# One-bank PSUM tiles in merging, four places for the decay weights, and earlier loads, in a hybrid encoder on one Trainium2 core

## The chip, the cores and the metric

The program runs on one core of a Trainium2 chip. The core has TensorE (PE, matrix products, with a separate sequence of weight loads, PEld), VectorE (DVE), ScalarE (ACT), GpSimd (POOL) and SyncE (SP), which here issues nearly all DMA transfers. The engines run their own instruction streams in order and wait for each other through semaphores. The metric is the device time of one execution in microseconds (us).

## What is computed

One layer of an encoder on 1024 prompt tokens and 256 sample tokens, with 1024 channels:

```python
h = rms_norm(x, norm_g) * (1.0 + scale) + shift          # scale, shift, gate from c @ w_ada
cb, cc, cx, cz, q, k, v, o, mz, gpre, gmerge = split_combined(h @ w_in)
y_conv = cb * centred_dwconv3(cc * cx, conv_w, conv_b) * silu(cz)
hm = mlstm_chunkwise(q, k, v, forward gates) + the same backward     # 4 heads of 256, chunks of 128
y_m = sigmoid(o) * head_rms_norm(hm) * silu(mz)
merged = g_conv * (y_conv @ w_proj_conv) + g_mlstm * (y_m @ w_proj_mlstm)   # gates: sigmoid(gmerge)
y = rms_norm(x + gate * (merged @ w_out), final_norm_g)
```

## The kernel before, in words

Matrix products run in fp32r with both factors split into a high and a low part: a product is three matmuls, high by high, high by low and low by high. ScalarE casts the high part of a weight (`wh`, from a loaded `raw` tile), and GpSimd subtracts it for the low part (`wl`); in the first stage that is L320 and L321, in the second L1665 and L1666.

The order of all work is planned on the host by a small class, `Board`. Code appends operations with an engine, an estimated cost, what they read and write, and sometimes marks: `low` (a load or product that goes behind the others), `slack` (its planned start is put later by so much). `order()` plans start times, at 230 KB/us for loads and a fixed landing time, and `play()` emits the instructions in the order of the planned starts. So one edit moves instructions on engines that it does not touch. Buffers of a pool are handed out in turn. Dependencies follow whole tiles: an engine that writes any part of a PSUM tile waits for a pending read of any other part.

There are four stages. (1) Up to about 1163 us the input projection (`go`, L810), by Strassen's scheme; results leave PSUM through `q` tiles on VectorE (L719). Within it the gates' recurrences and the decay weights of the mLSTM are worked out. `weights(i)`, called for 20 pieces, takes a `big` tile, loads two rows of log weights broadcast to all partitions (`big<-a_dr`, 256 KB), adds a mask on GpSimd (L1246), exponentiates on ScalarE (four times, L1250) and stores the result for the sweeps. (2) Up to about 1444 us the sweeps over the mLSTM's chunks (classes `Sweep` and `Pairs`). They leave gaps on TensorE, which `Filler` fills with the convolution branch's projection: 16 blocks of 128 channels and 640 tokens, two units each, of 24 matmuls 128x320 (L1707 to L1709). `load_w` loads raw weights for two blocks, `split` makes `wh` and `wl`, and VectorE multiplies the accumulator by the gate tile `th` (L620, inside `times_1p`). `load_head(h, n)` loads piece n of a head's `vN`, `qT` and `kT`. (3) Up to about 1566 us merging (`merge`): 16 blocks, two groups of 24 matmuls (L1883 to L1885) each. VectorE takes the group out of PSUM by L620 with a gate tile `th`, and adds the convolution's part (`zc`, L1891). At its beginning the second half of the mLSTM's output is loaded and split, on VectorE by L1850. (4) The output projection, again by Strassen's scheme, in two quads of token tiles and a last pair (class `Tokens`, products L1975 to L1977), with the norm at the end. PSUM has eight banks of 512 floats per partition; merging and the output have them as four tiles of two banks (`psD` one, `psO` three).

Of the kernel before, what the change touches and what calls it, by code (L numbers as in the profile page):

```python
# [182 lines left out]
def encoder_kernel(  # L183
# [1055 lines left out]

    def weights(i):  # L1240

        gx = gcol[:, 0].rearrange("p d h c -> p d (h c)")
        place = big()
        abc = (lambda: place[:, 0:4 * P].rearrange("p (d j s) -> p d j s", d=2, j=2))
        load(256, abc, a_rows[:, 2 * i:2 * i + 2, :].partition_broadcast(P), ["a_dr"], [place])
        op("POOL", 1.35, lambda: G.tensor_tensor(out=abc(), in0=abc(), in1=masks[:].unsqueeze(2).to_broadcast([P, 2, 2, P]),  # L1246
                                                 op=ALU.add), r=[place], w=[place])
# [5 lines left out]
        store(256, ex_dr[i], lambda: place[:, 0:4 * P], [place])  # L1253
# [172 lines left out]
    def load_head(h, n, which="qkv"):  # L1426

        i, (c0, c1) = h % 2, PIECES[n]
        hs, ts_ = slice(h * HD, (h + 1) * HD), slice(c0 * P, c1 * P)
        kb = 128 * (c1 - c0)  # L1430
        if "v" in which:
            load(kb, lambda: vNs[i][:, c0:c1, 0:HD], v_dr[ts_, hs].rearrange("(c p) d -> p c d", p=P), (), [(vNs[i], n)], h > 0)
        for nm, t, src in (("q", qTs[i], qT_dr), ("k", kTs[i], kT_dr)):
            if nm in which:
                load(kb, lambda t=t: t[:, :, ts_], src[hs, ts_].rearrange("(b p) t -> p b t", p=P), (), [(t, n)], h > 0)
# [207 lines left out]
    class Filler:  # L1643
# [36 lines left out]
        def unit(self, after):  # L1680
# [66 lines left out]
    for s in range(10 * NH + 15):  # L1747
# [62 lines left out]
    banks = []  # L1810

    def bank():
        k = len(banks)
        if k % 2 == 0:
            banks.append(buf(*((psO, [P, 2, 512], F32, "acc", 3) if k % 8 < 6 else (psD, [P, 2, 512], F32, "acc", 1))))
        else:
            banks.append(banks[-1])
        b = banks[-1]
        return (lambda: b[:, k % 2]), (b, k % 2)
# [48 lines left out]
    def merge(i, y):  # L1868
# [6 lines left out]
        for q in range(2):  # L1875
# [3 lines left out]
            def mm(part, acc=acc, qs=qs):  # L1879
                for kt in range(2 * part, 2 * part + 2):  # L1880
                    wh, wl = (w[:, kt % 4, :] for w in ws[kt // 4])
                    yH, yL = (t[:, kt % 4, qs] for t in y[kt // 4])
                    PE.matmul(acc()[:, :TQ], wh, yH, start=kt == 0, stop=False)  # L1883
                    PE.matmul(acc()[:, :TQ], wh, yL, start=False, stop=False)  # L1884
                    PE.matmul(acc()[:, :TQ], wl, yH, start=False, stop=kt == KT - 1)  # L1885
# [4 lines left out]
            op("DVE", .48, lambda acc=acc, qs=qs: times_1p(th[:, qs], th[:, qs], acc()[:, :TQ]), r=[tok, (th, q)], w=[(th, q)])  # L1890
# [15 lines left out]
    class Tokens:  # L1906
# [73 lines left out]
        def banks(self, pool):  # L1980
            b = buf(pool, [P, 2, 512], F32, "acc", 1 if pool is psD else 3)
            return [((lambda j=j: b[:, j]), (b, j)) for j in range(2)][:self.n]

        def copy_out(self, dst, tag):

            t = o_tile(tag)
            for j in range(self.n):
                ap, tok = dst[j]
                op("ACT", .57, lambda j=j, ap=ap: A.copy(t[:, j * 512:(j + 1) * 512], ap()), r=[tok], w=[(t, j)])
            return t  # L1990
# [117 lines left out]

    og = ctx.enter_context(tc.tile_pool(name="og", bufs=1))
# [42 lines left out]
    for st, nxt in ((quad0, quad1), (quad1, pair)):  # L2152
# [10 lines left out]
        c = st.banks(psO)  # L2163
# [28 lines left out]
        g = st.banks(psO)  # L2192
# [10 lines left out]
    banks_ = [buf(pool, [P, 2, 512], F32, "acc", 1 if pool is psD else 3) for pool in (psO, psO, psO)]  # L2203
    p0, p1, p2, _, *gb = [[((lambda t=t, i=i: t[:, i]), (t, i))] for t in banks_ for i in range(2)]
# [107 lines left out]
```

## Time and profile before

| | us |
|---|---|
| three runs | 1684.97, 1679.0, 1684.75 (median 1684.75) |
| profiled execution | 1680.08 |
| its span | 1678.3 |
| TensorE busy | 1628.0 (97%) |
| VectorE, ScalarE, GpSimd busy | 1026.3, 587.0, 700.4 |
| DMA moved | 274.41 MB, mean 164 GB/s |

TensorE's mean granted clock was 0.993 of full. A row of a timeline has start, length, engine, line, operation, output and inputs, and in brackets the idle time before it with what ended it. A row of waits names who waited, for what, the sum, how many times, and the longest.

### The profile page before, as it was taken

What the parts mean: (1) busy time and instruction counts of PE and PEld (TensorE: products, weight loads), DVE (VectorE), ACT (ScalarE), POOL (GpSimd) and SP (SyncE); (2) the same over time, 40 slices, a digit from 0 to 9 for tenths busy, and PEclk for the clock granted to TensorE, in tenths of its full rate; (3) what the DMA queues carried; (4) which work ended last, traced back from release to release, by engine and by line L of the source; (5) the groups of instructions that cost most, each with busy time, mean ns of one, the idle gap of its engine ahead of it and who ended that gap; (6) DMA issues with size and microseconds to landing.
All of it is one profiled execution on the core that took longest, in us unless ns stands there. A gap on an engine that the chain in (4) does not pass through costs nothing.

```text
span 1678.3 us, 28164 instructions
## 1 busy us (share of the span) xinstructions
PE 1628.0 (97%) x10504; PEld 1556.4 (93%) x10504; DVE 1026.3 (61%) x1747; ACT 587.0 (35%) x1172; POOL 700.4 (42%) x545
## 2 busy tenths in 40 slices
PE   6999999999999999999999999999999999999997
PEld 3989999999999999999999999999888889998876
DVE  5785655556564665566666886652157778533587
ACT  4643443323444322222222212121256665311232
POOL 1243676623455666667666643333210001333000
PEclk8999999999999999999999999999999999999999
DMA  9434778811445322222222565558878865794654
GB/s 360 128 101 147 231 239 229 219 55 59 128 133 152 94 70 70 83 71 63 63 73 69 142 142 133 124 132 260 287 249 256 275 193 167 258 347 160 225 190 162
DMA packets 310524, 274.41 MB, mean 164 GB/s; under 512 B 98820, under 2 KB 260852, under 8 KB 310388
## 3 DMA queue, kind: packets, MB, share of 16 engines
q1 hardware_dynamic: 310084, 272.35, 52.7%
q8 instruction: 83, 1.36, 0.3%
q14 instruction: 53, 0.43, 0.1%
q10 hardware_dynamic: 304, 0.27, 0.0%
HBM read 186.89 MB, written 85.66 MB: 162 GB/s over the span
## 4 chain that ended last, share of the span: by engine, by line
PE 87%; DMA 5%; DVE 3%; issue 1%; ACT 1%; SPq 1%; POOL 1%; DVEq 0%; POOLq 0%; ACTq 0%
PE acc L810 59%; PE u L1500 3%; PE qc L1460 3%; PE acc L1883 2%; PE acc L1885 2%; PE acc L1884 2%; PE acc L1975 2%; PE acc L1977 2%; PE acc L1976 2%; PE acc L1708 2%; PE acc L1707 2%; PE acc L1709 2%; DMA raw<-in_w_in_dram 2%; PE misc L1583 1%; PE misc L1543 1%
## 5 line engine op out<-in xcount | busy, mean ns | idle before, releaser
L321 POOL TENSOR_TENSOR wl<-comb,wh 128x512 fp32r<-128x512 f32 x176 | 246.5, 1401 | 243.8 <-ACT wh L320 223.5
L321 POOL TENSOR_TENSOR wl<-raw,wh 128x512 fp32r<-128x512 f32 x168 | 233.5, 1391 | 274.4 <-ACT wh L320 269.1
L719 DVE TENSOR_TENSOR q<-acc,q 128x640 f32<-128x640 f32 x272 | 220.6, 818 | 185.8 <-PE acc L810 175.4
L810 PE MATMUL acc<-xt,wh 128*128 128x320 f32 x1408 | 263.9, 309 | 0.0
L810 PEld LDWEIGHTS acc<-xt,wh 128*128 128x128 f32 x1408 | 220.9, 188 | 0.1
L320 ACT CAST wh<-raw 128x512 fp32r<-128x512 f32 x168 | 103.7, 619 | 319.5 <-PE acc L810 184.4
L320 ACT CAST wh<-comb 128x512 fp32r<-128x512 f32 x176 | 108.8, 619 | 271.8 <-PE acc L810 237.9
L810 PE MATMUL acc<-xt,wl 128*128 128x320 f32 x704 | 160.5, 309 | 0.0
L1666 POOL TENSOR_TENSOR wl<-raw,wh 128x512 fp32r<-128x512 f32 x28 | 36.0, 1288 | 227.4 <-ACT wh L1665 219.0
L810 PEld LDWEIGHTS acc<-xt,wl 128*128 128x128 f32 x704 | 117.7, 188 | 0.0
L675 DVE TENSOR_TENSOR comb<-raw 128x512 f32<-128x512 f32 x88 | 72.9, 829 | 65.4 <-DMA raw<-in_w_in_dram 41.6
L878 POOL TENSOR_TENSOR big<-big,q 128x640 f32<-128x640 f32 x48 | 78.6, 1638 | 35.3 <-DVE q L719 26.9
L620 DVE SCALAR_TENSOR_TENSOR th<-th,acc 128x320 f32<-128x320 f32 x62 | 30.1, 486 | 101.1 <-PE acc L1885 55.0
L617 ACT ACTIVATE q<-q,zero 128x640 f32<-128x640 f32 x76 | 63.0, 830 | 70.2 <-DVE q L719 69.3
L810 PE MATMUL acc<-b10H,wh 128*128 128x320 f32 x352 | 81.4, 313 | 3.4 <-DVE q L719 3.4
L810 PE MATMUL acc<-t3L,wh 128*128 128x320 f32 x352 | 81.2, 312 | 2.7 <-DVE t3L L372 2.7
L675 DVE TENSOR_TENSOR comb<-raw,comb 128x512 f32<-128x512 f32 x44 | 48.1, 1092 | 58.2 <-POOL wl L321 58.2
L810 PE MATMUL acc<-t3H,wh 128*128 128x320 f32 x352 | 81.2, 312 | 1.4 <-ACT t3H L371 1.4
L810 PE MATMUL acc<-b00H,wh 128*128 128x320 f32 x352 | 82.5, 316 | 0.0
L810 PE MATMUL acc<-t2H,wh 128*128 128x320 f32 x352 | 80.5, 310 | 1.6 <-DVE q L719 1.6
L810 PE MATMUL acc<-t3H,wl 128*128 128x320 f32 x352 | 81.1, 312 | 0.1
L810 PE MATMUL acc<-b11H,wh 128*128 128x320 f32 x352 | 81.2, 312 | 0.0
(392 smaller groups left out, 4159.9 us busy)
## 6 DMA issues: line engine op xcount, KB each, us to landing
raw<-in_w_in_dram SPq DMA_DIRECT2D x120, 256.0 KB
raw<-in_w_in_dram SPq DMA_DIRECT2D x34, 512.0 KB
th<-th_dr SPq DMA_DIRECT2D x31, 320.0 KB
th_dr<-q SPq DMA_DIRECT2D x28, 320.0 KB
raw<-in_w_proj_conv_dram SPq DMA_DIRECT2D x16, 512.0 KB
raw<-in_w_proj_mlstm_dram SPq DMA_DIRECT2D x16, 512.0 KB
late<-t_dr SPq DMA_DIRECT2D x16, 512.0 KB
k<-kn_dr SPq DMA_DIRECT2D x56, 128.0 KB
```

Of the source, the lines that this page charges most:

```text
L320: op("ACT", .63, lambda: A.copy(wh[:], src()), r=r, w=[wh])
L321: op("POOL", 1.4, lambda: G.tensor_tensor(out=wl[:], in0=src(), in1=fp(wh[:]), op=ALU.subtract), r=[*r, wh], w=[wl])
L617: A.activation(out, in_, AF.Tanh, bias=zero[:, 0:1], scale=0.5)
L675: op("DVE", .9, lambda: V.tensor_tensor(out=t[:], in0=x(), in1=y(), op=o), r=[x.tok, y.tok], w=[t])
L719: op("DVE", .82, lambda: V.tensor_tensor(out=two(dst()), in0=acc[:, :, 0:TQ], in1=two(t()), op=ALU.add), r=[acc, t.tok], w=[dst.tok])
L810: PE.matmul(acc[:, q, 0:TQ], st_[:, k_, :], m_[:, q * TQ:(q + 1) * TQ], start=k_ == 0 and n == 0, stop=k_ == 3 and n == 2)
L878: op("POOL", 1.65, lambda: G.tensor_tensor(out=dst(), in0=dst(), in1=t(), op=ALU.mult), r=[dst.tok, t.tok], w=[dst.tok])
L1460: PE.matmul(pq[:, 0:HD + 2], qTs[i][:, kd, c * P:(c + 1) * P], C[:, kd, :], start=kd == 0, stop=kd == 1)
L1500: PE.matmul(pu[:, db, 0:HD + 2], k[:, db * P:(db + 1) * P], wv[:], start=True, stop=True)
L1666: op("POOL", 1.36, lambda wh=wh, wl=wl, src=src: G.tensor_tensor(out=wl[:], in0=src(), in1=fp(wh[:]), op=ALU.subtract), r=[raw, wh], w=[wl])
L1707: PE.matmul(acc[:, :TQ], wh, yH, start=kt == 0, stop=False)
L1708: PE.matmul(acc[:, :TQ], wh, yL, start=False, stop=False)
```

## The change

It has five parts.

1. `weights` uses four places, the two halves of two `big` tiles that it keeps, for its pieces in turn, where it took a `big` tile for each piece. The mask's addition on GpSimd has a slack of 4 us.
2. `load_head` is called without the `low` mark at steps 3 and 5 of the sweeps, which load the second head and the rest of the first head's keys.
3. `Filler.unit` asks for the gate tile of block i + 1 when block i starts, ahead of the next weights. Before, it asked for block i's own tile there, behind them.
4. Merging has four one-bank tiles of its own (`psY`), one for each group. Two two-bank tiles (`psO`) stand beside them; for the output there come two more (`psE` and `psD`). In the last pair the groups `p0`, `p1`, `p2` and the two of `gb` have a tile each, where `p0` and `p1` shared one and the two of `gb` another.
5. `copy_out` copies a quad's two banks by one instruction of 1024 elements, where there were two of 512.

```diff
@@ weights(i)
-        place = big()
-        abc = (lambda: place[:, 0:4 * P].rearrange("p (d j s) -> p d j s", d=2, j=2))
+        if not weighing:
+            weighing.extend(big() for _ in range(2))
+        b, c = weighing[i % 2], i // 2 % 2
+        place = (b, c)
+        abc = (lambda: b[:, c * 4 * P:(c + 1) * 4 * P].rearrange("p (d j s) -> p d j s", d=2, j=2))
...
-                                                 op=ALU.add), r=[place], w=[place])
+                                                 op=ALU.add), r=[place], w=[place], slack=4.0)
@@ load_head and its call
-    def load_head(h, n, which="qkv"):
+    def load_head(h, n, which="qkv", low=True):
...
-            load(kb, lambda: vNs[i][:, c0:c1, 0:HD], ..., h > 0)
+            load(kb, lambda: vNs[i][:, c0:c1, 0:HD], ..., low and h > 0)
...
         if s in (3, 5):
             for h, n in ((0, 0), (1, 2), (1, 1)) if s == 3 else ((1, 0), (0, 1)):
-                load_head(h, n, "qkv" if h else "k")
+                load_head(h, n, "qkv" if h else "k", False)
@@ Filler.unit, at a block's start
+                if i < 2 * KT - 1:
+                    b1, n1 = divmod(i + 1, KT)
+                    t0 = HBS[b1][0]
+                    self.th[i + 1] = buf(thp, [P, TH2], F32, "th", NTH)
+                    load(320, lambda i=i: self.th[i + 1][:], th_dr[n1 * P:(n1 + 1) * P, t0:t0 + TH2], (), ...)
                 if i % 2 == 0 and i < 2 * KT - 2:
                     self.load_w(i // 2 + 1)
...
-                if i:
-                    self.th[i] = buf(thp, [P, TH2], F32, "th", NTH)
-                    load(320, lambda i=i: self.th[i][:], th_dr[n * P:(n + 1) * P, t0:t0 + TH2], (), ...)
@@ merging's pools
-    psD, psO = (ctx.enter_context(tc.tile_pool(name=nm, bufs=n, space=PSUM)) for nm, n in (("psD", 1), ("psO", 3)))
+    psO = ctx.enter_context(tc.tile_pool(name="psO", bufs=2, space=PSUM))
+    psY = hpstack.enter_context(tc.tile_pool(name="psY", bufs=4, space=PSUM))
     def bank():
-        k = len(banks)
-...
+        b = buf(psY, [P, 512], F32, "acc", 4)
+        return b, b
@@ the output
+    psE, psD = (ctx.enter_context(tc.tile_pool(name=nm, bufs=1, space=PSUM)) for nm in ("psE", "psD"))
-            for j in range(self.n):
-                ap, tok = dst[j]
-                op("ACT", .57, lambda j=j, ap=ap: A.copy(t[:, j * 512:(j + 1) * 512], ap()), r=[tok], w=[(t, j)])
+            ap, toks = self.both(dst)
+            op("ACT", .57 * self.n, lambda: A.copy(self.tile(t), ap()), r=toks, w=[(t, j) for j in range(self.n)])
-        c = st.banks(psO)
+        c = st.banks(psE)
-        g = st.banks(psO)
+        g = st.banks(psE)
-    banks_ = [buf(pool, [P, 2, 512], F32, "acc", 1 if pool is psD else 3) for pool in (psO, psO, psO)]
-    p0, p1, p2, _, *gb = [[((lambda t=t, i=i: t[:, i]), (t, i))] for t in banks_ for i in range(2)]
+    p0, p1, p2, *gb = [st.banks(pool) for pool in (psO, psO, psE, psD, psO)]
```

The order of the instructions shows what the planner makes of it, at three places. In the first, merging, this is TensorE's stream about the odd group of one of the later blocks (`acc` with its number is a PSUM tile, `y0` and `y1` are high and low part of the mLSTM's output, `waits DVE` a wait for VectorE). Before:

```order
L1885 MATMUL acc_15844<-y2_15003,wl_15793 128x320
L1883 MATMUL acc_15844<-y0_14526,wh_15758 128x320
L1884 MATMUL acc_15844<-y1_14715,wh_15758 128x320
L1885 MATMUL acc_15844<-y0_14526,wl_15767 128x320
L1883 MATMUL acc_15844<-y0_14526,wh_15758 128x320
L1884 MATMUL acc_15844<-y1_14715,wh_15758 128x320
L1885 MATMUL acc_15844<-y0_14526,wl_15767 128x320
L1883 MATMUL acc_15844<-y0_14526,wh_15758 128x320 [waits DVE_49]
```

The group's first six matmuls go without a wait, and the seventh, at its second quarter, waits for VectorE's read of the even group. After:

```order
L1883 MATMUL acc_15834<-y2_14978,wh_15772 128x320
L1884 MATMUL acc_15834<-y3_15025,wh_15772 128x320
L1885 MATMUL acc_15834<-y2_14978,wl_15781 128x320
L1883 MATMUL acc_15874<-y0_14508,wh_15754 128x320 [waits DVE_49]
L1884 MATMUL acc_15874<-y1_14565,wh_15754 128x320
L1885 MATMUL acc_15874<-y0_14508,wl_15762 128x320
```

The even group's last matmuls and the odd one's first three: the odd group has another tile, and its wait for VectorE stands on its first matmul.

The second place is GpSimd's stream from the first of the decay weights on (`big<-big,masks` is a mask's addition, `wl` a weight's low part). Before:

```order
L1246 TENSOR_TENSOR big<-big,masks 128x512 x2
L321 TENSOR_TENSOR wl<-comb,wh 128x512 x2
L321 TENSOR_TENSOR wl<-raw,wh 128x512
L1246 TENSOR_TENSOR big<-big,masks 128x512
L321 TENSOR_TENSOR wl<-comb,wh 128x512
L1246 TENSOR_TENSOR big<-big,masks 128x512
L321 TENSOR_TENSOR wl<-raw,wh 128x512 x2
```

After, where the additions stand five lines further down in the file:

```order
L1251 TENSOR_TENSOR big<-big,masks 128x512 x4
L321 TENSOR_TENSOR wl<-comb,wh 128x512
L321 TENSOR_TENSOR wl<-raw,wh 128x512
L321 TENSOR_TENSOR wl<-comb,wh 128x512
L321 TENSOR_TENSOR wl<-raw,wh 128x512
L1251 TENSOR_TENSOR big<-big,masks 128x512
L321 TENSOR_TENSOR wl<-raw,wh 128x512
L1251 TENSOR_TENSOR big<-big,masks 128x512 x2
```

Four additions stand together at first, and the fifth comes behind four splits.

The third place is SyncE's stream early in the sweeps, behind the loads of the first head (`vN`, `qT`, `kT` are a head's values, queries and keys, `k` keys by chunk, `zc_dr` a store of the filler, `raw` its weights for blocks 4 and 5). Before:

```order
L309 DMA kT<-kT_dr 128x2x640
L309 DMA th<-th_dr 128x640
L309 DMA k<-kn_dr 128x256 x2
L309 DMA kT<-kT_dr 128x2x384
L309 DMA th<-th_dr 128x640
L309 DMA k<-kn_dr 128x256 x2
L1718 DMA zc_dr<-raw 128x640
```

From these rows to the raw weights for blocks 4 and 5 there stand one more gate tile and three pairs of `abc` and `og` loads. After:

```order
L309 DMA kT<-kT_dr 128x2x640
L309 DMA vN<-v_dr 128x2x256
L309 DMA qT<-qT_dr 128x2x256
L309 DMA kT<-kT_dr 128x2x256
L309 DMA vN<-v_dr 128x3x256
L309 DMA qT<-qT_dr 128x2x384
L309 DMA kT<-kT_dr 128x2x384
L1724 DMA zc_dr<-raw 128x640
L309 DMA th<-th_dr 128x640
L309 DMA k<-kn_dr 128x256 x2
L309 DMA vN<-v_dr 128x5x256
L309 DMA qT<-qT_dr 128x2x640
```

Six loads of the second head now stand ahead of the second `k` pair, and the last two rows are the first two of three more, of five chunks each. The raw weights for blocks 4 and 5 come behind all nine, and behind the same `abc` and `og` loads.

More of the change, by code (lines that the diff above doesn't have):

```diff
@@ L1238, in thirds @@
         return finish
+    weighing = []
     def weights(i):
         gx = gcol[:, 0].rearrange("p d h c -> p d (h c)")
-        place = big()
-        abc = (lambda: place[:, 0:4 * P].rearrange("p (d j s) -> p d j s", d=2, j=2))
+        if not weighing:
[3 more added lines that the diff above has]
+        abc = (lambda: b[:, c * 4 * P:(c + 1) * 4 * P].rearrange("p (d j s) -> p d j s", d=2, j=2))
         load(256, abc, a_rows[:, 2 * i:2 * i + 2, :].partition_broadcast(P), ["a_dr"], [place])
         op("POOL", 1.35, lambda: G.tensor_tensor(out=abc(), in0=abc(), in1=masks[:].unsqueeze(2).to_broadcast([P, 2, 2, P]),
-                                                 op=ALU.add), r=[place], w=[place])
+                                                 op=ALU.add), r=[place], w=[place], slack=4.0)
         for d in range(2):
@@ L1252, in weights @@
                    r=[place, "pre"], w=[place])
-        store(256, ex_dr[i], lambda: place[:, 0:4 * P], [place])
+        store(256, ex_dr[i], lambda: b[:, c * 4 * P:(c + 1) * 4 * P], [place])
     sts = {n: gate_pair(n, n + 2, max(i - 2, 0), i == 0) for i, n in enumerate((0, 1, 4, 5, 8, 9))}
@@ L1431, in load_head @@
         if "v" in which:
-            load(kb, lambda: vNs[i][:, c0:c1, 0:HD], v_dr[ts_, hs].rearrange("(c p) d -> p c d", p=P), (), [(vNs[i], n)], h > 0)
+            load(kb, lambda: vNs[i][:, c0:c1, 0:HD], v_dr[ts_, hs].rearrange("(c p) d -> p c d", p=P), (), [(vNs[i], n)], low and h > 0)
         for nm, t, src in (("q", qTs[i], qT_dr), ("k", kTs[i], kT_dr)):
             if nm in which:
-                load(kb, lambda t=t: t[:, :, ts_], src[hs, ts_].rearrange("(b p) t -> p b t", p=P), (), [(t, n)], h > 0)
+                load(kb, lambda t=t: t[:, :, ts_], src[hs, ts_].rearrange("(b p) t -> p b t", p=P), (), [(t, n)], low and h > 0)
     class Sweep:
@@ L1689, in unit @@
                     self.split(i + 1)
+                if i < 2 * KT - 1:
+                    b1, n1 = divmod(i + 1, KT)
+                    t0 = HBS[b1][0]
+                    self.th[i + 1] = buf(thp, [P, TH2], F32, "th", NTH)
+                    load(320, lambda i=i: self.th[i + 1][:], th_dr[n1 * P:(n1 + 1) * P, t0:t0 + TH2], (),
+                         [(self.th[i + 1], 0), (self.th[i + 1], 1)])
                 if i % 2 == 0 and i < 2 * KT - 2:
@@ L1693, in unit @@
                     self.load_y(1)
-                t0 = HBS[b][0]
-                if i:
-                    self.th[i] = buf(thp, [P, TH2], F32, "th", NTH)
-                    load(320, lambda i=i: self.th[i][:], th_dr[n * P:(n + 1) * P, t0:t0 + TH2], (),
-                         [(self.th[i], 0), (self.th[i], 1)])
             acc = buf(psF, [P, 512], F32, "acc", 2)
@@ L1804, in encoder_kernel @@
     bstack.close()
-    psD, psO = (ctx.enter_context(tc.tile_pool(name=nm, bufs=n, space=PSUM)) for nm, n in (("psD", 1), ("psO", 3)))
+    psO = ctx.enter_context(tc.tile_pool(name="psO", bufs=2, space=PSUM))
+    psY = hpstack.enter_context(tc.tile_pool(name="psY", bufs=4, space=PSUM))
     mgp = ctx.enter_context(tc.tile_pool(name="mgp", bufs=1))
     zcp = hpstack.enter_context(tc.tile_pool(name="zcp", bufs=5, side="right"))
-    banks = []
     def bank():
-        k = len(banks)
[L1814 to L1819, printed above, removed]
+        b = buf(psY, [P, 512], F32, "acc", 4)
+        return b, b
     def mg_half(pool, tags):
@@ L1882, in mm @@
                     yH, yL = (t[:, kt % 4, qs] for t in y[kt // 4])
-                    PE.matmul(acc()[:, :TQ], wh, yH, start=kt == 0, stop=False)
-                    PE.matmul(acc()[:, :TQ], wh, yL, start=False, stop=False)
-                    PE.matmul(acc()[:, :TQ], wl, yH, start=False, stop=kt == KT - 1)
+                    PE.matmul(acc[:, :TQ], wh, yH, start=kt == 0, stop=False)
+                    PE.matmul(acc[:, :TQ], wh, yL, start=False, stop=False)
+                    PE.matmul(acc[:, :TQ], wl, yH, start=False, stop=kt == KT - 1)
             for part in range(4):
@@ L1889, in merge @@
                 op("PE", .88, lambda part=part, mm=mm: mm(part), r=ops + ([tok] if part else []), w=[tok])
-            op("DVE", .48, lambda acc=acc, qs=qs: times_1p(th[:, qs], th[:, qs], acc()[:, :TQ]), r=[tok, (th, q)], w=[(th, q)])
+            op("DVE", .48, lambda acc=acc, qs=qs: times_1p(th[:, qs], th[:, qs], acc[:, :TQ]), r=[tok, (th, q)], w=[(th, q)])
             op("DVE", .49, lambda qs=qs: V.tensor_tensor(out=mg[:, n % 4, qs], in0=th[:, qs], in1=zc[:, qs], op=ALU.add),
@@ L1980, in banks @@
         def banks(self, pool):
-            b = buf(pool, [P, 2, 512], F32, "acc", 1 if pool is psD else 3)
+            b = buf(pool, [P, 2, 512], F32, "acc", 2 if pool is psO else 1)
             return [((lambda j=j: b[:, j]), (b, j)) for j in range(2)][:self.n]
```

## The prediction

> **What bounds the kernel.** I read the busy shares first, then stages of my own cutting, then who TensorE waits for, then the timelines at those places.
>
> ```profile
> PE 1628.0 (97%) x10504; PEld 1556.4 (93%) x10504; DVE 1026.3 (61%) x1747; ACT 587.0 (35%) x1172; POOL 700.4 (42%) x545
> ```
>
> TensorE is busy for 97% of the span of 1678.3 us. The change takes away no matmul, so it can win only out of the 50 us in which TensorE is idle, or works at a lower clock. The stages show where that lies (columns: window, length, PE, PEld, DVE, ACT, POOL busy with instructions, granted clock, DMA share, GB/s):
>
> ```profile
> 1163.00:1443.60 280.60, 271.12 (x1625) 248.92 (x1624) 174.78 (x580) 147.98 (x389) 41.09 (x36) 1.00 0.72 234
> 1443.60:1476.00 32.40, 32.40 (x222) 32.40 (x221) 13.89 (x20) 11.19 (x17) 13.06 (x10) 1.00 0.97 343
> 1476.00:1566.60 90.60, 84.22 (x553) 81.18 (x552) 32.20 (x59) 14.90 (x24) 28.34 (x20) 1.00 0.59 206
> 1652.40:1678.30 25.90, 16.67 (x94) 14.18 (x93) 19.31 (x49) 4.77 (x11) 2.58 (x2) 0.92 0.36 122
> ```
>
> Row one is the sweeps with the convolution's projection as filler, rows two and three are merging, row four is the tail after the quads, where VectorE is busier than TensorE. Merging loses nothing in its first 32 us and 6.4 us in the other 90. TensorE's waits in the whole run:
>
> ```profile
> PE acc L1883 <- DVE th L620: 6.4, 11, 0.6
> PE acc L810 <- DVE q L719: 5.0, 4, 3.4
> PE acc L1707 <- DVE th L620: 2.8, 1, 2.8
> PE u L1479 <- DMA kT<-kT_dr: 1.6, 1, 1.6
> PE acc L1975 <- ACT raw L1989: 1.4, 2, 0.7
> PE acc L1975 <- DVE raw L2239: 1.1, 1, 1.1
> PE acc L1975 <- DVE raw L2016: 0.8, 1, 0.8
> ```
>
> The seven rows sum to 19.1 us. Each part of the change touches one or two of them.
>
> **Merging: one-bank tiles.** Before, two groups of 24 matmuls share a tile, and the wait of the second stands in its midst. After, it stands on a group's first matmul, for a tile used four groups ago. When VectorE reads late that is worse, when it reads in time it is free. VectorE's reads (L620), for groups 0, 1, 4, 11, 12 and 13, and TensorE's starts of groups 4 and 5:
>
> ```profile
> 1460.52 0.49 DVE L620 SCALAR_TENSOR_TENSOR th<-th,acc 128x320 f32<-128x320 f32 x1 [0.23 <-DMA th<-th_dr]
> 1464.26 0.47 DVE L620 SCALAR_TENSOR_TENSOR th<-th,acc 128x320 f32<-128x320 f32 x1
> 1474.34 0.49 DVE L620 SCALAR_TENSOR_TENSOR th<-th,acc 128x320 f32<-128x320 f32 x1 [4.44 <-DMA th<-th_dr]
> 1483.50 0.49 DVE L620 SCALAR_TENSOR_TENSOR th<-th,acc 128x320 f32<-128x320 f32 x1 [1.25 <-PE acc L1885]
> 1487.01 0.49 DVE L620 SCALAR_TENSOR_TENSOR th<-th,acc 128x320 f32<-128x320 f32 x1 [2.50 <-PE acc L1885]
> 1491.42 0.49 DVE L620 SCALAR_TENSOR_TENSOR th<-th,acc 128x320 f32<-128x320 f32 x1 [3.40 <-PE acc L1885]
> 1457.69 0.31 PE L1883 MATMUL acc<-y,wh 128*128 128x320 f32 x1
> 1461.22 0.31 PE L1883 MATMUL acc<-y,wh 128*128 128x320 f32 x1
> 1484.04 0.42 PE L1883 MATMUL acc<-y,wh 128*128 128x320 f32 x1 [0.58 <-DVE th L620]
> ```
>
> A free group takes 1461.22 - 1457.69 = 3.53 us, a pair 7.06. From the eleventh group on a pair takes 1491.42 - 1483.50 = 7.92: 0.86 lost, more than the 0.58 of the wait, as the restart is slow. Eleven such pairs (the waits' count) make 9.4 us. With four tiles the read of group n must end before group n+4. Late in merging it ends some 10 us ahead, so the 9.4 us go. But group 0's read begins only at 1460.52, as its gate tile lands then; it ends at 1461.01, and TensorE starts 0.05 us after such a read (1484.04 after 1483.99). So group 4 starts at 1461.06 rather than 1457.69: 3.37 lost. Group 5 could start at 1464.59 and needs group 1's read, which ends at 1464.73: 0.19 more. Group 8 needs the read of 1474.34, over at 1474.83, and comes at 1475.4: free. The landings do not move, as DMA is at 0.97 there. Merging: 9.4 - 3.6 = 5.8, bounds 4.3 (clock, below) to 9.4.
>
> **Decay weights.** TensorE's longest wait of the first stage lies there. The chain of waits, and the clock after it:
>
> ```profile
> 494.95 5.91 DMA big<-a_dr
> 501.02 1.30 POOL big L1246
> ...
> 508.54 6.54 DMA raw<-in_w_in_dram
> ...
> 515.20 1.43 DVE comb L675
> 516.63 0.74 DVE q L719
> ...
> 517.51 2.74 PE acc L810 x9
> 517.50:521.00 3.50, 3.49 (x14) 3.50 (x15) 2.66 (x3) 2.46 (x6) 2.41 (x3) 0.56 0.26 73
> POOL big L1246 <- DMA big<-a_dr: 17.4, 5, 5.5
> ```
>
> GpSimd stands in front of L1246 until a row vector has landed; the weight splits behind it (L321) free their raw buffer late, the next raw load is late, VectorE waits for it, and the drain of q behind it on VectorE holds TensorE. After, four vectors are on their way at once, so GpSimd's 17.4 us of waits should go but for the first. It waits and 3.4 us go, with the lost clock, 3.5 x (1 - 0.56) = 1.5: 4.9. The other three waits of that row (5.0 - 3.4 = 1.6) are not on this chain, I leave them. On the other side four additions stand in one clump: 2 x 1.3 = 2.6 us later for the weight splits behind it. Bounds: -2.6 to 6.5; I take 4.9, as the chain names the load.
>
> **The sweeps' loads.** The gate tile asked for at once removes the 2.8, and the early kT the 1.6. But SyncE's queue now has nine loads of the second head, 3840 KiB, in front of the pair of raw weights of filler blocks 4 and 5, that unit 8 needs (first row below). Before, DMA shows 348 GB/s there:
>
> ```profile
> 1204.28 0.39 PE L1707 MATMUL acc<-b00H,wh 128*128 128x320 f32 x1
> 1180.00:1200.00 20.00, 19.25 (x120) 18.61 (x121) 5.04 (x9) 2.49 (x5) 0.00 (x0) 1.00 1.01 348
> 1180.21 0.89 DVE L620 SCALAR_TENSOR_TENSOR th<-th,acc 128x320 f32<-128x320 f32 x2 [9.68 <-DMA th<-th_dr]
> 1200.70 0.61 ACT L1665 CAST wh<-raw 128x512 fp32r<-128x512 f32 x1
> 1201.39 1.27 POOL L1666 TENSOR_TENSOR wl<-raw,wh 128x512 fp32r<-128x512 f32 x1 [21.95 <-ACT wh L1665]
> ```
>
> The pair of gate tiles queued early had landed by 1180.2. From there to the raw pair's end the queue held 5632 KiB (k six times 128, kT 640 and 384, gate tiles three times 320, a store of 320, abc and og six times 256, raw 1024), 5.77 MB: at 348 GB/s landed at 1196.8, before its cast at 1200.70. After it holds 9472 KiB, 9.70 MB, behind one more tile of 0.33 MB: 1180.2 + 0.9 + 27.9 = 1209. Its first half is there 1.5 us earlier, cast and split take 0.61 + 1.27, so unit 8 runs from about 1208.5 instead of 1204.3: -4.2, though 2.8 us of it are what the gate tile had won. Six sweep matmuls more stand ahead of it now (+0.9 behind it), the kT wait goes (+1.6), and an idle stretch of some 6 us should cost the clock once more (-1.5, the row above). Sum -3.2. Bounds: +4.4, if the pair lands by 1201, to -6.3, if DMA is a tenth slower.
>
> The Trainium skill, TensorE: Matmul & The Clock Gate, Part 1: The HAM clock gate, says that an idle window of about 3.4 us halves the clock until a busy window of about 3.4 us has passed, so it speaks against the change at group 4 of merging and at unit 8. The trace agrees after the 3.4 us wait (0.56). By that rule each place costs an estimated 1.7 us, and the sum would end at 1672.4.
>
> By this trace's rows the loss is 1.5 us, after a wait of 3.4 us; group 4's 3.37 us holds the restart too, its idle time is shorter, so the sum takes it for unit 8 alone.
>
> **Quads and the last pair.** One copy of 128x1024 in place of two of 128x512: TensorE had waited for the first while filling the tile's other half.
>
> ```profile
> 1569.44 0.39 PE L1976 MATMUL acc<-b,wh 128*128 128x512 f32 x1
> 1569.68 0.40 PE L1977 MATMUL acc<-b,wl 128*128 128x512 f32 x1
> 1570.75 0.50 PE L1975 MATMUL acc<-b,wh 128*128 128x512 f32 x1 [0.68 <-ACT raw L1989]
> 1664.01 0.69 DVE L2016 TENSOR_TENSOR raw<-acc,y 128x512 f32<-128x512 f32 x1 [0.26 <-PE acc L1977]
> 1670.96 0.42 DVE L2239 TENSOR_TENSOR raw<-acc,y 128x256 f32<-128x256 f32 x1 [0.20 <-PE acc L1977]
> ```
>
> 1.07 us between starts instead of 0.24 just before, twice: 1.7. In the last pair TensorE's waits of 0.8 and 1.1 go, but VectorE sets the end there, and waits for TensorE only 0.26 and 0.20: 0.4. Together 2.1, bounds 1.7 and 3.6.
>
> **Sum.** 5.8 + 4.9 - 3.2 + 2.1 = 9.6. The profiled execution took 1680.08 us (span and 1.8 around it), 4.7 under the median of 1684.75, and one run of three was 1679.0. 1680.1 - 9.6 = 1670.5, from the median 1675; I say 1671.
>
> **Rivals.** (1) DMA keeps up, unit 8 waits for nothing: the sweeps win 4.4 instead of losing 3.2: 1663. For it: the landing is worked out from a mean rate over 20 us. Against it: 9.7 MB in these 20 us would need 485 GB/s, so a part of it is likelier than the whole. (2) The decay weights bring nothing, since the order on GpSimd and SyncE is planned anew and another load is late: 1675. For it speaks that the raw load itself took 6.54 us, which nothing shortens. (3) Slower: the raw pair lands so late that it eats all. Without unit 8 the sum is 13.8; it is gone when the unit starts at 1218 (9.7 MB at 270 GB/s), and the kernel is 0.5% slower at 1226.5. Against it, 348 GB/s. (4) Merging does not do what it says: the early gate tiles are later still, group 4 waits 9 us, and the pairs' gain is used up: 1676. Against it, group 0's gate tile was there at 1460.52 with the same queue ahead of it.
>
> **Chances.** A measurement tells apart about 0.5%, 8.4 us. As summed, 1666 to 1675: 0.48; rival 1 wholly or in part, 1660 to 1666: 0.17; rival 2: 0.16; rival 4: 0.10; rival 3: 0.06; the rest lies about no change. Range 1660 to 1680. Faster by 0.5% (below some 1674): most of the first, all of rival 1: 0.6. Same: rivals 2 and 4 and the first's edge: 0.34. Slower: 0.06.
>
> **What would show it.** Right: no wait of L1883 for L620 but one of about 3.4 us at group 4, and a cadence of 3.53 us; no wait of TensorE between 500 and 520; a wait of several us at unit 8, for the cast or split of raw weights; no wait of L1975 for a copy. Wrong: unit 8 on time, a second wait in merging near groups 5 to 10, or GpSimd still held by the row vectors.

## The result and the profile after

The changed kernel takes 1674.53 us, the median of ten runs (1670.13 to 1677.7), the kernel before 1680.61 (1678.27 to 1684.97). The ratio is 0.9962, 95% interval 0.9948 to 0.9975: 6.1 us faster, which the interval tells from none, though it is under the 0.5% that the prediction took as its bound. It had 1671 in 1660 to 1680. The profiled execution took 1674.54 us, span 1672.8.

TensorE's busy time, and of its waits those that bear on the change, from the page and the view of waits. Others as long, at L248, L510 and L372, belong to the kernel's start and stand in both kernels; the prediction's seven rows leave them out too.

```profile
PE 1628.8 (97%) x10504; PEld 1561.2 (93%) x10504; DVE 1027.1 (61%) x1747; ACT 588.8 (35%) x1170; POOL 703.8 (42%) x545
```

```profile
PE acc L810 <- DVE q L719: 4.1, 2, 2.8
PE acc L1883 <- DVE th L620: 3.4, 1, 3.4
PE qc L1465 <- DVE C L1513: 2.8, 3, 0.9
PE misc L1585 <- DVE Pt L1582: 1.9, 1, 1.9
PE u L1505 <- DMA k<-kn_dr: 1.4, 1, 1.4
PE acc L1713 <- ACT wh L1670: 1.1, 1, 1.1
PE acc L1715 <- POOL wl L1671: 0.8, 1, 0.8
```

Of the seven rows of before, five are gone: the filler's gate tile (2.8), kT (1.6), the copies (1.4) and the pair's two (1.9 together). Merging's eleven waits of 6.4 us have become one of 3.4. The q row has 4.1 us instead of 5.0. New are waits of sweep steps (L1465, L1505) and of unit 8 (L1713 and L1715), and the one for Pt (L1585), 0.9 us before, has become 1.9.

To see where 5.5 us went, the span is cut at three matmuls: the filler's first, merging's first, the quads' first. Before and after, from TensorE's timelines:

```profile
1162.80 0.31 PE L1707 MATMUL acc<-b00H,wh 128*128 128x320 f32 x1
1443.56 0.31 PE L1883 MATMUL acc<-y,wh 128*128 128x320 f32 x1
1565.72 0.40 PE L1975 MATMUL acc<-b,wh 128*128 128x512 f32 x1
```

```profile
1161.00 0.31 PE L1713 MATMUL acc<-b00H,wh 128*128 128x320 f32 x1
1446.46 0.31 PE L1883 MATMUL acc<-y,wh 128*128 128x320 f32 x1
1564.28 0.39 PE L1975 MATMUL acc<-b,wh 128*128 128x512 f32 x1
```

| us | before | after | gain | predicted |
|---|---|---|---|---|
| first stage, to the filler's first matmul | 1162.8 | 1161.0 | 1.8 | 4.9 |
| sweeps, to merging's first | 280.8 | 285.5 | -4.7 | -3.2 |
| merging, to the quads' first | 122.2 | 117.8 | 4.3 | 5.8 |
| output, to the span's end | 112.6 | 108.5 | 4.1 | 2.1 |
| sum | 1678.3 | 1672.8 | 5.5 | 9.6 |

In merging the cadence is free, and one gap stands where it was expected, at group 4. The first three rows are that place in TensorE's timeline, the fourth the granted clock in the window behind it:

```profile
1460.44 0.31 PE L1885 MATMUL acc<-y,wl 128*128 128x320 f32 x1
1464.16 0.60 PE L1883 MATMUL acc<-y,wh 128*128 128x320 f32 x1 [3.41 <-DVE th L620]
1464.56 0.47 PE L1884 MATMUL acc<-y,wh 128*128 128x320 f32 x1
1464.20:1467.50 3.30, 3.30 (x14) 3.30 (x15) 3.30 (x3) 0.10 (x1) 2.75 (x2) 0.56 1.04 398
```

3.41 us idle, then the clock at half up to 1467.1 (0.56 is the mean of the window). Unit 8, and the issue of its raw weights, before in the first row and after in the others, with four windows of the changed kernel at the end:

```profile
1188.55 0.96 SPq L309 DMA_DIRECT2D raw<-in_w_proj_conv_dram  x2
```

```profile
1198.82 1.13 SPq L309 DMA_DIRECT2D raw<-in_w_proj_conv_dram  x2
1203.41 1.11 PE L1465 MATMUL qc<-C,qT 128*128 128x258 f32 x4 [0.94 <-DVE C L1513]
1206.32 1.11 PE L1465 MATMUL qc<-C,qT 128*128 128x258 f32 x4 [0.94 <-DVE C L1513]
1208.51 0.41 PE L1713 MATMUL acc<-b00H,wh 128*128 128x320 f32 x1 [1.07 <-ACT wh L1670]
1209.86 0.42 PE L1715 MATMUL acc<-b00H,wl 128*128 128x320 f32 x1 [0.79 <-POOL wl L1671]
1180.00:1200.00 20.00, 18.45 (x112) 17.18 (x112) 4.41 (x8) 2.97 (x6) 0.00 (x0) 1.00 1.07 373
1200.00:1210.00 10.00, 5.77 (x23) 3.99 (x24) 2.48 (x7) 3.48 (x7) 1.47 (x2) 1.00 1.00 340
1211.10:1214.50 3.40, 3.40 (x15) 3.40 (x14) 0.00 (x0) 0.00 (x0) 2.41 (x2) 0.50 0.67 212
1429.60:1433.00 3.40, 3.40 (x14) 3.21 (x13) 1.54 (x6) 1.51 (x4) 0.00 (x0) 0.51 0.77 256
```

The raw weights are issued at 1198.82, 10 us later than before, and unit 8 starts at 1208.51, with DMA at 373 and then 340 GB/s and the clock at 1.00. TensorE fills the time ahead of it with sweep steps that the planner put there, one after the other, each waiting 0.94 us for the step before it.

Behind these waits the clock falls all the same: from 1211.1 it is at half for 3.4 us, though no wait there was longer than 1.07 us. It falls once more from 1429.6, behind the wait of 1.9 us for Pt. TensorE is busy in both stretches and loses 1.7 us of work in each: 3.4 us together, where the sweeps became 4.7 longer. Before, the clock of the sweeps is at 1.00 throughout.

### The profile page after: what moved, and what is told of

Its sections match the earlier page's. It is cut to its first block, busy times and chain, and to the rows that moved or that the text cites. A ratio compares the mean times of both kernels' runs of the same rounds, so it can differ in the third digit from the quotient of the medians.

```text
span 1672.8 us, 28179 instructions
## 1 busy us (share of the span) xinstructions
PE 1628.8 (97%) x10504; PEld 1561.2 (93%) x10504; DVE 1027.1 (61%) x1747; ACT 588.8 (35%) x1170; POOL 703.8 (42%) x545
## 4 chain that ended last, share of the span: by engine, by line
PE 63%; DMA 3%; DVE 1%; SPq 1%; issue 0%; ACT 0%; POOL 0%; DVEq 0%; POOLq 0%; ACTq 0%
PE acc L810 38%; PE u L1505 3%; PE qc L1465 2%; PE acc L1883 2%; PE acc L1884 2%; PE acc L1885 2%; PE acc L1977 2%; PE acc L1975 2%; PE acc L1976 2%; PE acc L1715 2%; PE acc L1714 2%; PE acc L1713 2%; DMA th<-th_dr 2%; PE misc L1588 1%; PE misc L1548 1%; SPq L309 1%
```

## The experiments

Twelve kernels ran. The stages add up, and most of a stage is the same from run to run when its code is (merging took 122.14 to 122.17 us in four profiled executions with the old tiles), so each profile shows what a part does where it stands. The table has the profiled executions; the ratios are of timed runs.

| | first stage ends | sweeps | merging | output | ratio to before |
|---|---|---|---|---|---|
| before | 1162.8 | 280.8 | 122.2 | 112.6 | |
| after | 1161.0 | 285.5 | 117.8 | 108.5 | 0.9962 (0.9948 to 0.9975) |
| e1_low | 1161.2 | 280.7 | 119.8 | 108.4 | 0.9937 (0.9923 to 0.9950) |
| e2_merge8 | 1160.6 | 285.5 | 113.7 | 108.5 | 0.9944 (0.9931 to 0.9956) |
| e3_weights | 1163.2 | 281.6 | 122.2 | 112.5 | one run |
| e4_output | 1164.8 | 280.0 | 122.1 | 108.5 | one run |
| e5_th | 1161.3 | 281.9 | 122.2 | 112.6 | one run |
| e6_plain | 1154.9 | 284.2 | 118.0 | 108.5 | one run |
| best1 | 1162.3 | 281.4 | 113.7 | 108.6 | 0.9908 (0.9895 to 0.9921) |
| best2 | 1159.9 | 287.2 | 113.7 | 108.5 | 0.9947 (0.9935 to 0.9958) |
| e8_tiles | 1162.2 | 281.1 | 113.7 | 108.5 | 0.9930 (0.9915 to 0.9945) |
| e9_copies | 1166.2 | 281.8 | 113.8 | 108.7 | 0.9940 (0.9927 to 0.9954) |
| e11_four | 1158.0 | 281.0 | 113.7 | 108.7 | 0.9912 (0.9898 to 0.9926) |
| e12_two | 1160.3 | 282.3 | 113.8 | 108.7 | 0.9918 (0.9904 to 0.9932) |

The sweeps hold no stretch at half clock in before, e4_output and e8_tiles, one of 3.4 us in e1_low, e3_weights, best1, e9_copies, e11_four and e12_two, and two (in e5_th one behind the other) in the rest.

### Part 2 undone (e1_low)

```diff
-                load_head(h, n, "qkv" if h else "k", False)
+                load_head(h, n, "qkv" if h else "k")
```

> The changed kernel with part 2 undone: the second head's loads and the rest of the first head's keys are marked low again at steps 3 and 5; all else as changed. My theory: the sweeps, from the filler's first matmul to merging's first, took 280.8 us before and 285.5 after because nine loads stand ahead of the raw weights that unit 8 needs. Then unit 8 starts some 41 us after unit 0 here (47.5 after, 41.5 before), with no wait for a cast or split; the gate tile's 2.8 us stay won, the kT wait of 1.6 comes back, and the sweeps take 277 to 280 us; the whole 1666 to 1670 us. Rival: the sweeps' loss is the replanned order of sweep steps and filler units near their end (2.1 us wait at 1426): then they still take 283 or more though unit 8 is on time, and the whole is 1672 or more.

1670.2 us (1668.63 to 1671.92). The sweeps took 280.7 us, 4.8 less than with part 2, and unit 8 starts without a wait, 41.9 us after unit 0:

```profile
1202.41 1.03 PE L1505 MATMUL u<-wv,k 128*128 128x258 f32 x4
1203.09 0.50 PE L1713 MATMUL acc<-b00H,wh 128*128 128x320 f32 x1
...
1460.45 0.60 PE L1883 MATMUL acc<-y,wh 128*128 128x320 f32 x1 [4.29 <-DVE th L620]
1460.50:1465.50 5.00, 5.00 (x19) 5.00 (x20) 4.93 (x7) 1.54 (x3) 2.73 (x2) 0.50 0.98 346
```

So part 2 costs 4.8 us. With the second head's early loads unit 8 came 5.6 us later than here, and unit 9, behind the half clock, 8.1 us; the filler made a part of that up, so the end of the sweeps came 4.8 us later. (For the first head's keys the edit changes nothing: `load_head` puts only later heads behind, by `low and h > 0`.) But the sweeps did not fall below those of before, as I expected of the gate tile: that part of the theory fell, and e5_th shows why. And merging became 2.0 us longer than after. TensorE comes to group 4 4.6 us sooner, but VectorE's read of group 0, which waits for its gate tile, only 3.7 us sooner (1459.82 instead of 1463.53), so the idle time there grew to 4.29 us. The rest is the clock: it stayed at half until 1465.8, 5.4 us behind the wait (last row) instead of 2.9.

### Eight tiles in merging (e2_merge8)

```diff
-    psY = hpstack.enter_context(tc.tile_pool(name="psY", bufs=4, space=PSUM))
+    psY = hpstack.enter_context(tc.tile_pool(name="psY", bufs=8, space=PSUM))
```

The output's pools are opened behind merging.

> The changed kernel with eight one-bank tiles for merging in place of four; the output's pools are opened when merging's tiles are released. My theory: group 4 then needs no read of group 0, so the idle 3.4 us there and the 1.4 us at half clock behind it go, no other wait takes their place, and merging (first matmul to last) takes 112.5 to 113 us in place of 117.4; the whole 1669 to 1671 us. Rival A: VectorE, late by the gate tile, holds group 8 instead: a wait of 1 to 3 us there. Rival B: the quads' first products wait for the release of merging's tiles: about 1 us more behind the last group, the rest as in my theory.

1670.67 us (1669.9 to 1673.21), the sum as expected, and 112.8 us from merging's first to its last matmul. All waits of TensorE from merging's beginning to the quads':

```profile
PE acc L1974 <- ACT wh L1830: 0.6, 1, 0.6
PE acc L1882 <- DVE th L620: 0.6, 1, 0.6
```

No wait at group 4 nor at group 8, no fall of the clock, and merging is 4.1 us shorter than after. From first to last matmul it is 9.2 us shorter than before, where the prediction counted 9.4 for the eleven pairs. The first row stands where rival B put it, at the quads (the view names ScalarE's cast, which ended at 1559.70; VectorE's read of the last group ended at 1559.66), the second at merging's own beginning (for the read of the filler's last unit). The four one-bank tiles had thus cost 4.1 of the 8.4 us that one-bank tiles can give here (122.2 to 113.7).

### Part 1 alone (e3_weights), and the load itself made plain (e6_plain)

The first is the kernel before with the new `weights`.

> The kernel before with part 1 alone: four places for the decay weights and the slack. My theory: the first stage's gain comes from here alone. From the first matmul of the input projection to its last, 1133.5 us before and 1130.2 after; here 1130 to 1131, with TensorE's longest wait between 440 and 550 us under 3 us and no stretch at half clock. Rival: the gain there is start-up scatter or another part's replanning: 1133 or more. The other stages as before; the whole 1676 to 1680 us.

1681.32 us, one run. The first stage ended at 1163.2, and from the projection's first to its last matmul it took 1133.6 us: the rival. Its longest wait between 440 and 550 us is 3.3 us. All kernels with the new `weights` and the one load (six) end their first stage at 1159.9 to 1163.2, mean 1161.4, the four with the old one at 1161.3 to 1164.8, mean 1162.8: 1.4 us, within a scatter of 3.5. Counted from the projection's first matmul, which starts between 28.7 and 30.9 us, the means are 1131.1 and 1133.1: 1.9 us, within a scatter of 5. What is left there in the changed kernel (waits, and two issues of SyncE), and in e3:

```profile
DVE comb L675 <- DMA raw<-in_w_in_dram: 13.0, 3, 8.3
POOL big L1251 <- DMA big<-a_dr: 11.0, 6, 3.7
...
480.24 0.37 SPq L309 DMA_DIRECT2D big<-a_dr  x1
480.70 0.97 SPq L309 DMA_DIRECT2D raw<-in_w_in_dram  x2
```

```profile
PE acc L810 <- DVE q L719: 6.5, 2, 3.3
```

VectorE still waits for raw weights, up to 8.3 us for one load; GpSimd stands in front of the decay weights 11.0 us instead of 17.4, yet the raw weights come no sooner. Behind one of TensorE's longest waits there the clock is at half for 3.4 us in both, as it was before. DMA in that time, in 40 slices of the window 480 to 487 us of the changed kernel (busy tenths, then GB/s):

```profile
DMA  3100010223334345376799596767769999999999
GB/s 129 47 0 0 0 47 0 76 88 88 82 76 76 70 94 88 76 105 99 67 76 76 47 82 61 79 82 143 140 161 275 319 342 348 351 369 372 480 377 363
```

From the broadcast load's start on, some 3.5 us pass at 47 to 105 GB/s, and only then, with the raw weights issued 0.5 us behind it, does the rate rise to 350. VectorE uses these weights at 489.31, 8.6 us after their issue. So the load was replaced:

```diff
-        load(256, abc, a_rows[:, 2 * i:2 * i + 2, :].partition_broadcast(P), ["a_dr"], [place])
+        load(256, abc, w_proj_conv[0][0:P, 0:4 * P].rearrange("p (d j s) -> p d j s", d=2, j=2), ["a_dr"], [place])
```

> The changed kernel, but the decay weights' load of two rows, broadcast to 128 partitions (256 KB), is replaced by a plain load of 256 KB, 128 partitions by 512 numbers of a weight matrix; the mLSTM's weights are then not those of the computation, all else is the same. My theory: what was left of the first stage's loss (6.6 us too many between 440 and 550 after) comes because the broadcast load itself takes some 5 us of all DMA engines at 60 to 90 GB/s, and raw weights queued behind it land after 8 us. Then here raw loads land after 2 to 4 us, TensorE waits for VectorE's q at most 1 us between 440 and 550, and the first stage's products take 1126 to 1129 us (1130 to 1132 with the change). Rival: SyncE comes late to the raw loads, since it stands before stores of the exponentials, or VectorE and GpSimd are late by themselves: then the wait of about 3 us at 490 stays.

1667.33 us, one run. The first stage ended at 1154.9, 6.1 us sooner than after and outside the scatter; from the projection's first to its last matmul it is 1124.1 us, better than expected. Between 440 and 550 VectorE has no wait for raw weights, TensorE has no wait at all, and the clock does not fall:

```profile
440.00:550.00 110.00, 110.00 (x752) 110.00 (x751) 61.45 (x65) 57.25 (x128) 70.38 (x50) 1.00 0.48 154
```

The cause of the loss there is the broadcast load, not the places for its result. This is one run, and the plain load differs in two things at once: no DRAM row goes to 128 partitions, and the pieces are 2 KB long instead of 1 KB.

### The output parts alone (e4_output)

The kernel before with part 5 and `p0, p1, p2, *gb` in tiles of their own.

> The kernel before with part 5 and a tile for each group of the last pair, the four two-bank tiles as before. From merging's last matmul to the last of all it took 105.4 us before and 101.2 after. My prediction gave 2.1 of that: 1.7 in the quads and 0.4 in the pair, since VectorE sets the end. Theory now: TensorE's two stalls in the pair (0.9 and 1.2 us) set the end all the same, so 101 to 101.5 here. Rival: the pair's gain after has another cause (one VectorE addition that took 1.78 us before and 0.69 after, by chance): then 103 to 103.7 here, and that addition again above 1 us. The whole 1675 to 1678 us.

1677.24 us, one run; the output took 4.1 us less, as in the changed kernel (from merging's last matmul to the last of all 100.9 in both, 105.1 before), so the pair's tiles are worth as much as the copy. The addition of the rival was 0.69 us in all eleven kernels with these parts, and 1.78 in before, e3_weights and e5_th; so it is not chance. In before it begins 0.06 us behind one of GpSimd's and ends 0.55 behind it; in the changed kernel it begins 0.28 us ahead, and GpSimd's takes 1.57 instead of 1.29. Before, then after, from the timelines of VectorE and GpSimd:

```profile
1664.68 1.29 POOL L2148 TENSOR_TENSOR y<-y,fng 128x512 f32<-128x512 f32 x1 [8.57 <-ACT raw L2025]
1664.74 1.78 DVE L2020 TENSOR_TENSOR y<-y,raw 128x512 f32<-128x512 f32 x1
```

```profile
1660.38 0.69 DVE L2019 TENSOR_TENSOR y<-y,raw 128x512 f32<-128x512 f32 x1
1660.66 1.57 POOL L2148 TENSOR_TENSOR y<-y,fng 128x512 f32<-128x512 f32 x1 [8.57 <-ACT raw L2024]
```

### Part 3 alone (e5_th)

> The kernel before with part 3 alone: each gate tile of the filler asked for one block ahead. My prediction gave it 2.8 us. The sweeps took 280.0 to 281.6 us in three kernels that have them as before. Theory: the wait of 2.8 us at unit 4 goes and the rest stays, 277 to 278.5. Rival: another wait comes in its place, as in the changed kernel with part 2 undone, whose sweeps took 280.7 with that wait gone: TensorE is held by a later load (keys, kT) in the same full DMA queue, and by the sweep's own recurrence at its end: then 280 to 281.

1679.75 us, one run; the sweeps took 281.9, more than even the rival's 280 to 281. The wait of 2.8 is gone, and these came, in place of 1.6 for kT and 0.9 for Pt:

```profile
PE misc L1580 <- DVE Pt L1577: 1.9, 1, 1.9
PE u L1500 <- DMA k<-kn_dr: 1.0, 1, 1.0
PE u L1479 <- DMA kT<-kT_dr: 0.7, 1, 0.7
```

Keys are waited for in the same full queue, and at the end of the sweeps, where the filler has little left to give, a chain between VectorE and TensorE costs 1 us more, as in every profile with part 3. And behind this wait the clock falls. Before in the first two rows, e5_th in the third:

```profile
PE misc L1580 <- DVE Pt L1577: 0.9, 1, 0.9
1421.00:1435.00 14.00, 13.12 (x88) 12.26 (x87) 11.81 (x33) 8.52 (x24) 2.61 (x2) 1.00 0.41 145
1424.50:1430.20 5.70, 5.70 (x21) 5.52 (x22) 2.21 (x9) 2.07 (x6) 0.00 (x0) 0.50 0.51 172
```

All ten profiles with part 3 have a stretch at half clock between 1421 and 1435 us, of 3.4 us or, here, twice that; none of the four without part 3 has one. TensorE loses 1.7 us of work in a stretch of 3.4, and some 2.8 in the 5.7 of the last row, as much as the gate tile's wait was worth. That the stretch comes from the longer wait for Pt is read from these profiles; no run takes that wait away by itself.

### Combinations (best1, best2, e8_tiles)

best1 has the edits of e1_low and e2_merge8. best2 promotes one piece of the second head, 768 KiB (`n < 2 and h > 0` for the mark). e8_tiles has the PSUM parts alone, without 1, 2 and 3.

> The changed kernel with part 2 undone and eight one-bank tiles in merging. If the two are independent of each other: sweeps 280.7, merging 112.8, the end 101.7, so against 1670.2 with part 2 undone alone 6.8 less and 0.8 more: 1664.2 us, 1663 to 1666. Rival: the full DMA queue at merging's beginning holds group 8 now, since TensorE gets there earlier: merging 114 to 116, the whole 1666 to 1669.

1665.06 us (1663.77 to 1668.41): the two are independent, merging has no second wait. Its ratio is the lowest here, 0.9908; e11_four and e12_two below cannot be told from it.

> As best1, but of the second head one piece of two chunks (three loads, 768 KiB in place of 3840) goes ahead as in the change. Theory: unit 8 waits as many bytes as stand ahead of its raw weights: 768 KiB are 2.3 us at 348 GB/s, which the 4 us between landing and use before cover: unit 8 some 42 us after unit 0, and the wait for the first kT goes (1.1 us): sweeps 279 to 280.5, the whole 0 to 1.5 us under best1. Rival: the promotion as such replans the order and costs whatever its size: sweeps 283 or more.

1671.02 us (1670.24 to 1676.77). Unit 8 started 44.0 us after unit 0, 2.2 later than in best1, as 768 KiB at 348 GB/s would make it if nothing covered them; unit 12 stood equal again at 62.2. But the sweeps took 287.2: up to unit 16 they stand within 0.4 us of best1's (133.7 and 133.3 behind unit 0), and 5.5 us are lost behind it, in no wait that stands out (the stretch at half clock near 1430 is in both). That is the rival: this plan costs apart from the bytes. Which of its moves does it stays open, and whether some of part 2's 4.8 us is of this kind.

> The kernel before with the PSUM parts alone: eight one-bank tiles in merging (in place of four two-bank ones; the change has four one-bank tiles), the one copy of part 5, and a tile for each group of the last pair. Parts 1, 2 and 3 are left out. By the stages read so far: merging 122.0 to 112.8, the output 105.1 to 101.7, together 12.6 us, and nothing else: first stage and sweeps as before (to 1161 to 1165, and 280 to 282). So 1680.6 - 12.6 = 1668, 1666 to 1670; best1, which has parts 1 and 3 besides, took 1665.1, so these two are worth 1 to 4 us. Rival: parts 1 and 3 are worth nothing measurable: 1664 to 1666.

1668.56 us (1667.32 to 1672.83): as expected. The medians put it 3.5 us behind best1, which has parts 1 and 3 besides, but the intervals of the ratios overlap, and the profiled executions, the fastest of this kernel and the last but one of best1, have the same first stage and sweeps (1162.2 and 281.1 against 1162.3 and 281.4). Whether the two parts are worth anything stays open; no stage shows it.

### A cheaper broadcast (e9_copies, e11_four, e12_two)

All three are best1 with copies of the log weights in DRAM, each broadcast to a part of the partitions. e9 has four copies and four planned loads a piece:

```diff
-        load(256, abc, a_rows[:, 2 * i:2 * i + 2, :].partition_broadcast(P), ["a_dr"], [place])
+        for n in range(4):
+            load(64, lambda n=n: abc()[n * 32:(n + 1) * 32], a_rows[n, :, 2 * i:2 * i + 2, :].partition_broadcast(32), ["a_dr"], [place])
```

> As best1, but the 64 KB of log weights stand in DRAM four times, and each of four loads of 64 KB broadcasts one copy to 32 partitions, where one load of 256 KB broadcast a single copy to 128. Same bytes into the tile, same length of a piece; three issues more on SyncE for each of the 20 pieces. Theory 1: the broadcast is slow because 128 partitions read the same 2 KB; then four copies take about a quarter of the 5 us, raw loads behind them land in 3 to 4 us, the waits near 490 and 515 us go, the first stage ends 4 to 6 us earlier, the whole 1659 to 1662. Theory 2: it is slow for the size or shape of its pieces (1 KB each), whatever they read: then no change of the raw loads' landing, the 24 us of issues on SyncE come on top, and the whole is 1665 to 1670.

1671.5 us (1669.24 to 1673.94). The waits at 490 and 515 had gone, but one of 8.3 us stood at 556, at the next step of Strassen's scheme, where SyncE issued raw weights late. The order was another (at 478 us the raw weights are issued ahead of the broadcasts), so e11 kept best1's: the four loads are one operation of the planner.

> As best1, with the log weights four times in DRAM as in e9_copies, but the four loads of a piece planned as one operation of the old size, so that every instruction besides stands where best1 has it. In e9 the waits at 490 and 515 had gone, and a new one of 8.3 us at 556 had come, where SyncE reached a raw load late. Theory 1 (128 reads of one copy are slow; e9's new wait came from the planner's new order): no wait over 1 us between 440 and 560, the input projection's first to last matmul 1124 to 1128 us (best1 1131.3), the whole 1659 to 1662 us (best1 1665.1). Rival: three issues more per piece, 0.4 us each on SyncE, hold the raw loads as much as the slow broadcast did: a wait of 3 us or more near 490 or 515 or 550, the whole 1664 or more.

1666.07 us (1663.21 to 1671.2), the same as best1. Its profiled execution, the fastest of the six, has waits of 2.0 us at most and no fall of the clock between 420 and 580 us, and its projection took 1128.6 us (best1 1131.2), close to what theory 1 wanted; the timed runs do not bear that out. e12 has two copies.

> As e11_four with two copies and two loads of 128 KB a piece. Theory 1: the broadcast takes half as long as with one copy, some 2.5 us, with one issue more: raw loads land 2 to 3 us earlier than in best1, which takes most of the waits; first to last matmul of the projection 1125 to 1129 us, the whole 1660 to 1663. If it is the number of readers of one copy beyond some point, or SyncE's issues, that count, it falls outside e11's and best1's span: under both or over both.

1666.89 us (1665.06 to 1669.63), its projection 1130.9 us: best1 once more. In e11 the raw weights behind the broadcast came nearly as late as with one copy, used 7.5 us after their issue where best1 has 8.6:

```profile
480.58 0.95 SPq L309 DMA_DIRECT2D raw<-in_w_in_dram  x2
488.06 0.69 DVE L675 TENSOR_TENSOR comb<-raw 128x512 f32<-128x512 f32 x1 [7.95 <-DMA raw<-in_w_in_dram]
```

So theory 1 fell in this form: a quarter of the readers for each copy does not bring the raw weights much sooner. Whether it is the 1 KB pieces, or copies that lie 64 KB apart in DRAM and so are no relief, stays open.

## Why the prediction came out as it did

The total lies in the range, 3.5 us above the value; the direction held, at two thirds of the size. Some of that is luck: merging, the sweeps and the decay weights fell short by 6.1 us together, and the output, by a step that failed, gave 2.0 more than forecast. By its own steps:

- **Merging.** Mechanism and place were right: no wait but at group 4, 3.41 us against 3.37. The size was off by 1.5: I held the idle time to be short of what lowers the clock, and the clock fell to half. Eleven matmuls from 1464.16 took 3.0 us where 1.6 would do. The bound named for that case, 4.3, is the measured gain. The rule of the Trainium skill (TensorE: Matmul & The Clock Gate, Part 1: The HAM clock gate), half the clock after an idle window of about 3.4 us until a busy one has passed, gave the prediction an estimated 1.7 us for this place and for unit 8, and a sum of 1672.4. Both prices came, 1.4 us here and 1.7 there, and the trace agrees with the length, 3.4 us at half clock each time. It does not show the condition as the prediction took it: at unit 8 no idle time of 3.4 us stood ahead of the fall.
- **Unit 8.** The mechanism was right: the raw weights came 10 us later, and unit 8 waited for their cast and split. It was forecast for 1208.5 and came at 1208.51, and that is luck. The first stage had ended 1.8 us sooner and DMA moved 373 GB/s between 1180 and 1200, not 348, yet counted from unit 0 it came 6.0 us later than before, not 4.2. The price of the clock came too, 1.7 us for a forecast 1.5, though not behind one stretch of some 6 us: the waits are five of 0.8 to 1.1 us, between sweep steps and in unit 8. Undoing part 2 takes waits and fall away, 4.8 us for it all; best2 leaves open how much of it is the order and not the bytes.
- **The gate tile and kT.** The step that counted 2.8 and 1.6 as won failed. Both waits went and others took their place (e5_th): 1.0 for keys and 0.7 for kT, in a queue that has no room (1.01 of the DMA engines' time before, 1.07 after, between 1180 and 1200), and 1.0 more for Pt at the end of the sweeps. Behind that last wait came the half clock, a loss of 1.7 us in the changed kernel, which the sum had at nothing.
- **Decay weights.** This is the term that was mis-sized most: 4.9 forecast, 1.4 (or 1.9, counted from the projection's first matmul) within the scatter shown. In the changed kernel a wait of 2.8 us ending at 493.4 and half clock from 494.3 took the place of those that the prediction counted as gone. The chain of waits named the broadcast load, 5.91 us, and the raw load, 6.54 us; I took the first for a wait in front of GpSimd. It was a transfer that keeps the raw load behind it, and no place for its result changes that, as e6_plain shows. Rival 2 had the right reason ("the raw load itself took 6.54 us"), and a chance of 0.16.
- **Output.** The copy gave its 1.7. The pair gave 2.4 more (the stalls before 1653.22 and 1668.20 cost 1.0 and 1.3), not 0.4, since the step "VectorE sets the end there" failed: VectorE was busy with work that nobody waited for (L2068), while its chain came through TensorE, from the read at 1652.47 over the products to the one at 1664.01. An idle time of 0.26 us in front of an instruction says how late its last input is, not how early it could be had. e4_output shows the 4.1 by itself.

## What to carry to other kernels

When half a buffer is traded for twice as many, look where its reader is late for another reason: the new wait costs its length, and here mostly a clock at half for 3.4 us behind it. That came behind one wait of 3.4 us, but also behind one of 1.9 and behind five of about 1 us, so read the granted clock past the end of a wait, not only up to it. In a transfer queue that is full, moving a load forward is a trade and not a gain; ask what stands behind it. And a wait that ends with a transfer may be cured neither by more places nor by asking sooner, if the transfer itself is slow: time it by itself first.

## What the runs showed of the hardware

Loads of 256 KB that broadcast rows of a DRAM tensor to all partitions ran at 47 to 105 GB/s for some 3.5 us, and the raw weights issued 0.5 us behind one were used 8.6 us after their issue; with a plain load of the same size in the same place VectorE waited for no raw weights there.

The length of an idle time alone did not decide whether TensorE's clock fell. In e3_weights two waits of 3.26 us, 25 us apart, stood for the same engine; behind the first the clock stayed at 1.00, behind the second it fell to half for 3.4 us:

```profile
493.71 0.53 PE L810 MATMUL acc<-t2H,wh 128*128 128x320 f32 x2 [3.26 <-DVE q L719]
493.71:497.11 3.40, 3.40 (x23) 3.40 (x24) 2.61 (x4) 3.40 (x9) 0.28 (x1) 1.00 0.75 195
518.32 0.53 PE L810 MATMUL acc<-b10H,wh 128*128 128x320 f32 x2 [3.26 <-DVE q L719]
519.40:522.80 3.40, 3.40 (x15) 3.40 (x14) 3.37 (x5) 2.89 (x8) 2.49 (x2) 0.50 0.46 174
```

In the changed kernel the stretches at half clock began at 494.3, 1211.1, 1429.6 and 1463.7 us, which are 210, 64 and 10 times 3.41 us apart. So the clock seems to change only on a fixed beat, and where a wait falls on it would count; no run tests that.

VectorE's 128x512 addition took 1.78 us when GpSimd's addition had begun 0.06 us sooner, and 0.69 when it began first, GpSimd's then 1.57 instead of 1.29, though the trace shows neither waiting for the other.
